# Layer 0's second feed-forward product as 60 slabs and 16 plain quads, with layer 1's memory keys and values right behind it

## The chip, the cores and the metric

One core of one Trainium2 chip. The metric is the device time of one execution in microseconds (us). The time before is the median of three runs.

The engines are PE (TensorE matmuls; PEld are its weight loads), DVE (VectorE), ACT (ScalarE), POOL (GpSimd) and SP (SyncE, which here only issues DMAs).

## The reference

A trunk of two layers over 256 tokens of width 2048, with a memory of 256 tokens, all in float32. What matters here:

```python
for i in range(DEPTH):
    if i == N_A_LAYERS:                       # layer 1
        sk1, sk2, sv = shared_kv(x, kv_norm, w_kv, k_norm, cos, sin)
    u = rms_norm(x, mix_norm[i]) @ w_in[i]
    ...                                       # pooling mixer (0) or differential attention (1)
    mem_out = memory_cross_attention(mem_q, mem, mem_norm[i], w_mem_kv[i], mem_q_norm[i], mem_k_norm[i])
    x = x + jnp.concatenate([token_out, mem_out], axis=-1) @ w_out[i]
    x = x + squared_relu_mlp(rms_norm(x, ffn_norm[i]), w_ff1[i], w_ff2[i])

def squared_relu_mlp(h, w1, w2):              # w1: 2048 x 8192, w2: 8192 x 2048
    z = jax.nn.relu(h @ w1)
    return (z * z) @ w2
```

The keys and values of the memory, `rms_norm(mem) @ w_mem_kv[i]`, need nothing of `x`. The shared keys and values of layer 1 need the `x` that layer 0's feed-forward part leaves.

## The kernel before, in words

**Numbers as high and low halves.** Every float32 operand is split into a rounded high half and the rest. A product is three matmuls: low x high, high x high, high x low. Weights come from HBM in the order of their use. ACT casts a block into `hi_ring`, and DVE subtracts that from the block into `lo_ring` (`_split`, L177 and L180). The rings have six places of 512 columns. `Feed.fill` prepares blocks up to three jobs ahead of PE; `Feed.load` issues the reads some loads ahead, from SP, into `raw` (four buffers, two quads each).

**Forms of a product.** A weight block is 128 x 128; a quad is four of them.
- `a_part`: the weight block is stationary, 256 tokens (high and low half, 512 columns) stream past it, then the low block with 256 columns (L434, L436).
- `wide_step`: a quad streams, and the tokens are stationary: 2 x 3 matmuls of 512 columns (L468 to L470).
- slabs: a slab is two row blocks of the second feed-forward matrix by eight column blocks. It is multiplied by a scheme of seven products in place of eight (L867 to L870), into seven PSUM banks `p`. Its four jobs hold 2, 1, 2 and 2 products. Job 0 takes a block as it is. Then POOL issues a DMA that adds other weights from HBM onto the block in place (`add_right`, L152), and job 1 takes this sum; a sum of L205 gives job 2; after job 2 there is another adding DMA and a sum of L219 for job 3. `product` also takes sums of the inputs (`sit`), made by DVE and ACT from two finished up tiles (`convert`, `combine`, L793 to L804).

**The feed-forward part** (`ffn`, once for a layer). 64 up tiles (`a_part`, 16 blocks each) make `z`, which keeps 16 of 64 row blocks. The slabs run between the up tiles: each job has a due time in up tiles (`tiles_at`), and `due` runs what is due at the start of each tile and after its 4th, 8th and 12th block. The right half of the columns is `g` = 0, the left half `g` = 1. The seven banks hold one side at a time, so the slabs go four on one side, then four on the other, and `swap` copies the banks out and in with ACT (L934, L926). Before, 56 slabs are used: all 32 of the right side, and 24 of the left. The left side is closed in the midst of the up tiles (`close_left`), scaled, and transposed into `resid` (`turn_left`). The rest of the left side, row blocks 48 to 63, follows behind the up tiles as eight down tiles (`down_tile`, `a_part` with 16 blocks each); the last 12 slab jobs run two at a time between them (`last`). `finish_banks` closes the right side and transposes it into `resid`. Each finished block of `resid` is split into `x_kv`.

**Then layer 1:** three tiles of k (`w_kv`), three of v, two of the memory (`mk1`, `mv1`), three of q, and four of the memory's queries with the heads of the attention between. Each tile of k, v, the memory and q is 16 `wide_step`s. The memory's input is read again while k and v run (`mem_again`: four DMAs of four blocks each through `raw`), and split into `mems1`.

**The order of the work.** `at(d, fn)` runs `fn` d ticks later; a tick is one quad, or one job in `last`. The framework that builds the kernel may place an instruction of an engine ahead of others in the code, when its inputs are there; `order` ties those together that have to stay in order.

Of the kernel before, what the change touches and what calls it, by code (L numbers as in the profile page):

```python
# [10 lines left out]
F32 = mybir.dt.float32  # L11
# [89 lines left out]
class Feed:  # L101
# [191 lines left out]
def program(ctx, tc, plan, dry, xT, memT, par, lam, cst, wst, yT):  # L293
# [160 lines left out]

    def wide_step(ps, what, xs, k):
        hi, lo = feed.quad(what)
        x = [(xs[:, k, t * P : t * P + P], xs[:, k, T + t * P : T + t * P + P]) for t in range(2)]
        if what[:2] == ("w_mem_kv", 0) and k < 2:

            for t in range(2):  # L460
                nc.tensor.matmul(ps[t], x[t][0], hi, start=k == 0, stop=False)
            for t in range(2):
                nc.tensor.matmul(ps[t], x[t][1], hi, start=False, stop=False)
            for t in range(2):
                nc.tensor.matmul(ps[t], x[t][0], lo, start=False, stop=False)
        else:
            for t in range(2):
                nc.tensor.matmul(ps[t], x[t][1], hi, start=k == 0, stop=False)  # L468
                nc.tensor.matmul(ps[t], x[t][0], hi, start=False, stop=False)  # L469
                nc.tensor.matmul(ps[t], x[t][0], lo, start=False, stop=k == NK - 1)  # L470
        feed.used(4)
        tick()
# [236 lines left out]

    def later_square(n):  # L710

        if n == 0:
# [17 lines left out]

    def ffn(l, xs, tags, done):

# [20 lines left out]
        cnt = [0]  # L753
        z_done, sit_done, summed_up = set(), set(), set()
        z_free = {j: True for j in range(NK)}
        sit_free = [True] * 4
# [180 lines left out]

        left = {}
        turns = []

        def close_left(j):

# [13 lines left out]
            else:  # L956
                u, v = left["u"], left["v"]
                add(u, u, banks[5])
                sub(v, v, u)
                add(u, u, banks[6])  # L960
            for p in of_job[j]:
                restore(p, 0)
            if j == 3:
                rows = ((left["c11"], 0), (left["c12"], 0), (u, 1), (v, 1))
# [83 lines left out]
        def one_job():  # L1048
# [40 lines left out]
        due(64)  # L1089
        assert len(jobs) == 12 and not turns  # L1090
        feed.loads_ahead = LOADS
# [21 lines left out]

        return last

# [222 lines left out]

    x_in = []
    down = ffn(0, fx, ("S1", "S0"), lambda n: resid_done(n, [(x_in[0], G_KV)], False))  # L1340
# [17 lines left out]

    mems1 = sp.tile([P, NK, 512], F32R, tag="S1", name="mems1")

    def mem_again(p):
        t = wp.tile([P, 4, T], F32, tag="raw", bufs=4, name="memraw1")
        nc.sync.dma_start(t, memT[:, 4 * p : 4 * p + 4, :])
        for k in range(4):
            at(
                6 + 2 * k,
                lambda k=k: split_gain(mems1[:, 4 * p + k, :], t[:, k, :], gcol(G_MEM + 16 + 4 * p + k)),
            )
# [8 lines left out]

    def pair_of_banks(c, name):
        if c % 2:
            return [pp.tile([P, 512], F32, tag="s", bufs=2, name=name) for _ in range(2)]  # L1380
        return [mmt(name) for _ in range(2)]

    c1 = []
    at(12, lambda: c1.extend(columns("x")))
    for c in range(3):
# [20 lines left out]
    mqg1 = mem_gain(1)  # L1406
    ps = pair_of_banks(0, "mk1")
    b_tile(ps, "w_mem_kv", 1, 0, mems1)
    mrow1 = key_rows(ps, mem_c, P)
    ps = pair_of_banks(1, "mv1")  # L1410
    b_tile(ps, "w_mem_kv", 1, 1, mems1)
    cat1 = sp.tile([P, NK, 512], F32R, tag="S1", name="cat1")

    mk1_lo = cat1[:, 12:16, 0:T]
    mv1_lo = cat1[:, 12:16, T : 2 * T].rearrange("p h (a d) -> p h a d", a=2)
    mv1 = tp.tile([P, 2, 512], F32R, tag="rows", bufs=3, name="mv1")
    mk1 = tp.tile([P, 4, T], F32R, tag="rows", bufs=3, name="mk1")
    for t in range(2):
        four = "p (h d) -> p h d"
        hi, v4 = mv1[:, t, :].rearrange(four, h=4), ps[t].rearrange(four, h=4)  # L1420
        split_rows(hi, mv1_lo[:, :, t, :], v4, mem_c[0][:, t : t + 1])
    for i in range(2):
        c = slice(2 * i, 2 * i + 2)
        at(
            2,
            lambda i=i, c=c: turn_rows(mrow1, 2 * i, mk1[:, c, :], gcol(G_MK + 1), mk1_lo[:, c, :]),
        )

    off = [1024]
# [235 lines left out]
```

## Time and profile before

| | |
|---|---|
| median of the runs | 1997.94 us (1997.89 to 1998.28) |
| profiled execution | 1997.9 us, span 1996.1 us |
| granted clock of PE | 1.00 |
| busy: PE, PEld | 1990.8 us (100%), 1704.1 us (85%) |
| busy: DVE, ACT, POOL | 1716.3 us (86%), 1497.9 us (75%), 246.5 us (12%) |
| DMA | 420.10 MB, mean 210 GB/s |

The profile is one execution, and times are counted from its span's start. Ends of matmuls are modelled, so their starts are read. A row of groups has: line, engine, operation, out<-in, count, then busy us and mean ns of one, then the idle time before them and what ended it. A row of the timeline has: start us, us, engine, line, operation, count. A row of DMA issues ends with the KB of each and the us from issue to landing.

Stages: layer 0's up tiles end at about 863 us; the down tiles end at about 926 us; k, v and the memory's tiles follow, and end at about 1101 us.

### The profile page before, as it was taken

The numbers are of one execution on the slowest core, as the hardware profiler recorded it, in microseconds if no ns is written. First come the engines' busy times: TensorE is split into PE (matmuls) and PEld (weight loads), VectorE is DVE, ScalarE is ACT, GpSimd is POOL, SyncE is SP. The second block draws the span as 40 slices with busy tenths as digits, with TensorE's granted clock in tenths as the row PEclk, the third lists the DMA queues.
The fourth block names the chain that finished last, engine by engine and source line by source line (L and its number), as shares of the span: only waits on it lengthen the run. The fifth ranks groups of instructions, "written<-read, shape, count | busy, mean of one in ns | idle before, by whom it ended". The sixth has DMA issues, their size and how long they took to land.

```text
span 1996.1 us, 32052 instructions
## 1 busy us (share of the span) xinstructions
PE 1990.8 (100%) x10534; PEld 1704.1 (85%) x10534; DVE 1716.3 (86%) x3089; ACT 1497.9 (75%) x2791; POOL 246.5 (12%) x291
## 2 busy tenths in 40 slices
PE   9999999999999999999999999999999999999999
PEld 8888888888888888888888888888888888888888
DVE  8888878889989899989765698878889898999987
ACT  7765577787887878778665699567787878878775
POOL 0001311111111111110000000311111111111110
PEclk9999999999999999999999999999999999999999
DMA  8556567888888888765576534657888888888775
GB/s 321 173 192 191 189 200 212 226 227 236 229 229 222 225 236 234 218 189 183 187 234 196 169 127 138 201 186 210 230 219 234 229 227 226 227 234 234 218 216 145
DMA packets 142727, 420.10 MB, mean 210 GB/s; under 512 B 16096, under 2 KB 18784, under 8 KB 142560
## 3 DMA queue, kind: packets, MB, share of 16 engines
q1 hardware_dynamic: 110160, 359.32, 55.3%
q0 software_dynamic: 32256, 58.73, 17.2%
q8 instruction: 82, 1.34, 0.3%
q14 instruction: 85, 0.70, 0.1%
q10 hardware_dynamic: 144, 0.01, 0.0%
HBM read 415.90 MB, written 2.10 MB: 209 GB/s over the span
## 4 chain that ended last, share of the span: by engine, by line
PE 99%; ACT 0%; DVE 0%; issue 0%
PE x_bank L434 25%; PE x_bank L436 12%; PE p L867 9%; PE p L869 9%; PE p L870 9%; PE wo L434 6%; PE wo L436 3%; PE u L434 2%; PE ff L434 2%; PE u L436 1%; PE q L468 1%; PE q L470 1%; PE k L468 1%; PE k L469 1%; PE q L469 1%; PE v L469 1%
## 5 line engine op out<-in xcount | busy, mean ns | idle before, releaser
L177 ACT CAST hi_ring<-raw 128x512 fp32r<-128x512 f32 x1001 | 613.5, 620 | 272.3 <-PE x_bank L434 69.2
L180 DVE TENSOR_TENSOR lo_ring<-raw,hi_ring 128x512 fp32r<-128x512 f32 x1001 | 686.4, 694 | 122.2 <-ACT hi_ring L177 106.2
L434 PE MATMUL x_bank<-fx,hi_ring 128*128 128x512 f32 x1952 | 610.1, 394 | 0.0
L436 PEld LDWEIGHTS x_bank<-fx,lo_ring 128*128 128x128 f32 x1952 | 366.6, 188 | 83.6
L436 PE MATMUL x_bank<-fx,lo_ring 128*128 128x256 f32 x1952 | 383.5, 278 | 0.0
L434 PEld LDWEIGHTS x_bank<-fx,hi_ring 128*128 128x128 f32 x1952 | 319.8, 189 | 24.0
L177 ACT CAST hi_ring<-room 128x1024 fp32r<-128x1024 f32 x224 | 236.0, 1053 | 128.1 <-PE p L869 107.4
L180 DVE TENSOR_TENSOR lo_ring<-room,hi_ring 128x1024 fp32r<-128x1024 f32 x224 | 274.0, 1223 | 37.7 <-ACT hi_ring L177 29.2
L180 DVE TENSOR_TENSOR lo_ring<-slab,hi_ring 128x512 fp32r<-128x512 f32 (+1 forms) x224 | 213.8, 954 | 60.3 <-ACT hi_ring L177 59.8
L177 ACT CAST hi_ring<-slab 128x512 fp32r<-128x512 f32 (+1 forms) x224 | 185.9, 831 | 40.3 <-PE p L869 23.9
L867 PE MATMUL p<-hi_ring,sit 128*128 128x512 f32 x448 | 175.5, 392 | 0.0
L869 PE MATMUL p<-hi_ring,sit 128*128 128x512 f32 x448 | 175.1, 391 | 0.0
L870 PE MATMUL p<-lo_ring,sit 128*128 128x512 f32 x448 | 174.3, 389 | 0.0
L152 POOL DMA_DIRECT2D room<-in_w x112 | 96.7, 863 | 556.3 <-DVE lo_ring L180 435.3
L152 POOL DMA_DIRECT2D slab<-in_w x112 | 96.8, 864 | 529.0 <-DVE lo_ring L180 521.1
L434 PE MATMUL wo<-cat,hi_ring 128*128 128x512 f32 x512 | 161.8, 397 | 0.3 <-DVE rc L405 0.3
L867 PE MATMUL p<-hi_ring,z 128*128 128x512 f32 x336 | 132.1, 393 | 0.0
L869 PE MATMUL p<-hi_ring,z 128*128 128x512 f32 x336 | 131.2, 390 | 0.0
L870 PE MATMUL p<-lo_ring,z 128*128 128x512 f32 x336 | 130.8, 389 | 0.0
L436 PEld LDWEIGHTS wo<-cat,lo_ring 128*128 128x128 f32 x512 | 95.9, 188 | 22.0
L436 PE MATMUL wo<-cat,lo_ring 128*128 128x256 f32 x512 | 101.5, 279 | 0.0
L870 PEld LDWEIGHTS p<-lo_ring,sit 128*128 128x128 f32 x448 | 84.2, 188 | 18.6
(375 smaller groups left out, 3369.7 us busy)
## 6 DMA issues: line engine op xcount, KB each, us to landing
raw<-in_w SPq DMA_DIRECT2D x500, 512.0 KB, 4.4
slab<-in_w SPq DMA_DIRECT2D x112, 512.0 KB, 4.7
room<-in_w SPq DMA_DIRECT2D x112, 256.0 KB, 4.7
slab<-in_w POOLq DMA_DIRECT2D x112, 256.0 KB, 6.6
room<-in_w POOLq DMA_DIRECT2D x112, 256.0 KB, 5.8
memraw<-in_mem SPq DMA_DIRECT2D x5, 512.0 KB, 4.2
resid<-in_x SPq DMA_DIRECT2D x8, 256.0 KB, 5.3
out_y<-resid SPq DMA_DIRECT2D x16, 128.0 KB, 1.9
```

The source lines that it names most:

```text
L152: self.nc.gpsimd.dma_start(t, self.wst[h, :, 0:512], accum_op=ALU.add)
L177: self.last_cast = self.nc.scalar.copy(hi, src)
L180: low = self.nc.vector.tensor_sub(lo, src, hi.bitcast(F32))
L434: nc.tensor.matmul(ps, hi, xs[:, k, :], start=first and c == 0, stop=False)
L436: nc.tensor.matmul(ps[:, T : 2 * T], lo, xs[:, k, 0:T], start=False, stop=last and c == len(ks) - 1,)
L468: nc.tensor.matmul(ps[t], x[t][1], hi, start=k == 0, stop=False)
L469: nc.tensor.matmul(ps[t], x[t][0], hi, start=False, stop=False)
L470: nc.tensor.matmul(ps[t], x[t][0], lo, start=False, stop=k == NK - 1)
L867: nc.tensor.matmul(ps, a[1], hi, start=new, stop=False, **again)
L869: nc.tensor.matmul(ps, a[0], hi, start=False, stop=False, **again)
L870: nc.tensor.matmul(ps, a[0], lo, start=False, stop=end, **again)
```

## The change

In layer 0 (`full`), the left side gets four more slabs, so there are 60: the right side's slabs 24 to 27 come with those of the left side, and the right side's 28 to 31 come last. The due times behind slab 50 follow each other by 0.9 up tiles, not by 1.7. `due` doesn't keep 12 jobs back; what isn't due by the 64th tile runs behind the up tiles, one job after the other (`last_full`). The left side's sums are closed after its slab 27 and kept; the rest of the left side, row blocks 56 to 63, follows behind the slabs as 16 plain quads (`wide_step`) in two pairs of banks, which are added to the kept sums and then scaled and transposed (`turn_side`). The right side is closed by `close_left` too, into `right`. Layer 1's feed-forward part stays as it was.

Behind that, the two tiles of layer 1's memory keys and values come ahead of k and v. Their input is read again while the plain quads run, into the places of `z` (`refill`). `load` returns early where three slabs' halves of one kind are still held.

```diff
@@ Feed.load
             r = self.plan.loads[self.lp]
+            if r[0] == "S" and sum(x[0] == "S" and x[2] == r[2] for x in self.raw) == 3:
+                return
@@ ffn
-        slabs += [(0, i, False) for i in range(24, 32)]
+        if full:
+            slabs += [(0, i, True) for i in range(24, 28)]
+            slabs += [(1, i, False) for i in range(24, 28)]
+            slabs += [(1, i, True) for i in range(28, 28)]
+            slabs += [(0, i, False) for i in range(28, 32)]
+        else:
+            slabs += [(0, i, False) for i in range(24, 32)]
...
-            return p + 8.4 if p <= 50 else 58.4 + 1.7 * (p - 50)
+            return p + 8.4 if p <= 50 else 58.4 + (0.9 if full else 1.7) * (p - 50)
...
-            if end and s + 1 < len(slabs):
-                if g == 1 and i == 23:
+            if s + 1 == len(slabs):
+                if full:
+                    at(1, lambda: close_left(j, right))
+            elif end:
+                if g == 1 and i == (28 - 1 if full else 23):
                     at(1, lambda: close_left(j))
...
-            while len(jobs) > 12:
+            while len(jobs) > (0 if full else 12):
...
+        def turn_side(side, base, h):
+            t4 = pp.tile([P, 2, T], F32, tag="ot"[h % 2], bufs=1, name="ct")
+            sides = ((side["c11"], side["c12"]), (side["u"], side["v"]))
+            ...
+            c = base + 2 * h
+            nc.vector.tensor_add(resid[:, c : c + 2, :], resid[:, c : c + 2, :], t4)
+            at(1, lambda: done(c))
+            at(2, lambda: done(c + 1))
+
+        def last_full():
+
+            while jobs:
+                one_job()
+                tick()
+            rest = range(56, 64)
+            n = len(rest)
+            for d, c, t in ((1, "c11", 0), (2, "c12", 0), (3, "u", 1), (4, "v", 1)):
+                at(d, lambda c=c, t=t: scale_rows(right[c], t))
+            for h in range(4):
+                at((5, 6, 8, 10)[h], lambda h=h: turn_side(right, 8, h))
+            refill(z, n)
+            for c in range(2):
+                ps = pair_of_banks(c, "ff2")
+                for k in rest:
+                    wide_step(ps, ("w_ff2", l, k, c, 4), z, k % NK, (rest[0] % NK, 63 % NK))
+
+                def close(c=c, ps=ps):
+                    for t in range(2):
+                        x = left[(("c11", "c12"), ("u", "v"))[t][c]]
+                        nc.vector.tensor_add(x, x, ps[t])
+                        at(1 + t, lambda x=x, t=t: scale_rows(x, t))
+
+                at(1, close)
+                for e in range(2):
+                    at(5 + e, lambda h=2 * c + e: turn_side(left, 0, h))
+
+        return last_full if full else last
@@ program, between the layers
+    def refill(z, n):
+        mems_in.append(z)
+        def again(p):
+            t = wp.tile([P, 4, T], F32, tag="raw", bufs=RAWS, name="memraw1")
+            nc.sync.dma_start(t, memT[:, 4 * p : 4 * p + 4, :])
+            for k in range(4):
+                at(4 + k, lambda k=k: split_gain(z[:, 4 * p + k, :], t[:, k, :], gcol(G_MEM + 16 + 4 * p + k)))
+        for p, d in enumerate((1, 7, 4 * n // 2 - 3, 4 * n // 2 + 1)):
+            at(d, lambda p=p: again(p))
...
     down()
-    for n in range(NK):
-        at(2 + n // 2, lambda n=n: later_square(n))
+    mems1 = mems_in[0]
+    for i, n in enumerate((8, 9, 10, 11, 12, 13, 14, 15, 0, 1, 2, 3, 4, 5, 6, 7)):
+        at(10 + i, lambda i=i, n=n: later_square(n, i == 0))
+    ps = pair_of_banks(0, "mk1")
+    b_tile(ps, "w_mem_kv", 1, 0, mems1)
+    ...                         # mk1, mv1 and what is made of them, moved from behind v
-    for p in range(4):
-        at(46 + 9 * p, lambda p=p: mem_again(p))
...
-    at(12, lambda: c1.extend(columns("x")))
+    at(2, lambda: c1.extend(columns("x")))
```

More of the change, by code (lines that the diff above doesn't have):

```diff
@@ L453, in c_tile, with wide_step @@
                 tick()
-    def wide_step(ps, what, xs, k):
+    def wide_step(ps, what, xs, k, ends=(0, NK - 1)):
         hi, lo = feed.quad(what)
@@ L467, in wide_step @@
             for t in range(2):
-                nc.tensor.matmul(ps[t], x[t][1], hi, start=k == 0, stop=False)
+                nc.tensor.matmul(ps[t], x[t][1], hi, start=k == ends[0], stop=False)
                 nc.tensor.matmul(ps[t], x[t][0], hi, start=False, stop=False)
-                nc.tensor.matmul(ps[t], x[t][0], lo, start=False, stop=k == NK - 1)
+                nc.tensor.matmul(ps[t], x[t][0], lo, start=False, stop=k == ends[1])
         feed.used(4)
@@ L708, in add_square, with later_square @@
         nc.gpsimd.tensor_add(acc[key], acc[key], sq)
-    def later_square(n):
-        if n == 0:
+    def later_square(n, first):
+        if first:
             acc["x"] = tp.tile([P, T], F32, tag="acc", bufs=1, name="acc")
@@ L728, in resid_done, with pair_of_banks, ffn @@
             add_square("x", resid[:, n, :], n == 0)
-    def ffn(l, xs, tags, done):
+    def pair_of_banks(c, name):
+        if c % 2:
+            return [pp.tile([P, 512], F32, tag="s", bufs=2, name=name) for _ in range(2)]
+        return [mmt(name) for _ in range(2)]
+    def ffn(l, xs, tags, done, refill=None):
         z = sp.tile([P, NK, 512], F32R, tag=tags[0], name=f"z{l}")
@@ L936, in swap, with close_left @@
                 restore(p, g)
-        left = {}
+        left, right = {}, {}
         turns = []
-        def close_left(j):
+        def close_left(j, left=left):
             add, sub = nc.vector.tensor_add, nc.vector.tensor_sub
@@ L960, in close_left @@
                 add(u, u, banks[6])
+            if left is right:
+                return
             for p in of_job[j]:
                 restore(p, 0)
-            if j == 3:
+            if j == 3 and not full:
                 rows = ((left["c11"], 0), (left["c12"], 0), (u, 1), (v, 1))
@@ L1089, in ffn @@
         due(64)
-        assert len(jobs) == 12 and not turns
+        assert full or len(jobs) == 12 and not turns
         feed.loads_ahead = LOADS
@@ L1343, in program @@
     down()
-    for n in range(NK):
-        at(2 + n // 2, lambda n=n: later_square(n))
+    mems1 = mems_in[0]
[3 more added lines that the diff above has]
+    b_tile(ps, "w_mem_kv", 1, 0, mems1)
+    mrow1 = key_rows(ps, mem_c, P)
+    ps = pair_of_banks(1, "mv1")
+    b_tile(ps, "w_mem_kv", 1, 1, mems1)
+    cat1 = sp.tile([P, NK, 512], F32R, tag="S1", name="cat1")
+    mk1_lo = cat1[:, 12:16, 0:T]
+    mv1_lo = cat1[:, 12:16, T : 2 * T].rearrange("p h (a d) -> p h a d", a=2)
+    mv1 = tp.tile([P, 2, 512], F32R, tag="rows", bufs=3, name="mv1")
+    mk1 = tp.tile([P, 4, T], F32R, tag="rows", bufs=3, name="mk1")
+    for t in range(2):
+        four = "p (h d) -> p h d"
+        hi, v4 = mv1[:, t, :].rearrange(four, h=4), ps[t].rearrange(four, h=4)
+        split_rows(hi, mv1_lo[:, :, t, :], v4, mem_c[0][:, t : t + 1])
+    for i in range(2):
+        c = slice(2 * i, 2 * i + 2)
+        at(
+            2,
+            lambda i=i, c=c: turn_rows(mrow1, 2 * i, mk1[:, c, :], gcol(G_MK + 1), mk1_lo[:, c, :]),
+        )
     x_mx = sp.tile([P, NK, 512], F32R, tag="S0", name="x_mx")
@@ L1357, in program @@
     ]
[L1359 to L1368, printed above, removed]
-    for p in range(4):
-        at(46 + 9 * p, lambda p=p: mem_again(p))
     ktab = rope_tables(G_KR, "krope")
@@ L1406, in program @@
     mqg1 = mem_gain(1)
[L1407 to L1427, printed above, removed]
     off = [1024]
```

21 lines of the change are left out of this document (14 added, 7 removed).

## Prediction

> **What bounds the kernel now.** I read the profile's page first: the span, the engines' busy time, and the chain of work that ended last.
>
> ```profile
> span 1996.1 us, 32052 instructions
> PE 1990.8 (100%) x10534; PEld 1704.1 (85%) x10534; DVE 1716.3 (86%) x3089; ACT 1497.9 (75%) x2791; POOL 246.5 (12%) x291
> PE 99%; ACT 0%; DVE 0%; issue 0%
> ```
>
> PE is busy all the time and holds 99% of the chain. A modelled matmul end can hide a wait, so the starts on the timeline of PE decide:
>
> ```profile
> 603.62 0.40 PE L867 MATMUL p<-hi_ring,sit 128*128 128x512 f32 x1
> ...
> 605.67 0.39 PE L867 MATMUL p<-hi_ring,sit 128*128 128x512 f32 x1
> ...
> 606.36 0.62 PE L434 MATMUL x_bank<-fx,hi_ring 128*128 128x512 f32 x2
> ...
> 608.43 0.40 PE L434 MATMUL x_bank<-fx,hi_ring 128*128 128x512 f32 x1
> ```
>
> From 603.62 to 605.67 lie nine 512-wide matmuls of the slab products, one every 0.228 us, though each is printed with 0.39 us. From 606.36 to 608.43 lie three pairs of `a_part` blocks, 0.69 us a pair, 0.345 us a block. PE starts a matmul as soon as the last has streamed, so any time in which a weight block comes late adds to the span. Then the busy time by stages (columns: us, then busy us of PE, PEld, DVE, ACT, POOL, clock, DMA share, GB/s):
>
> ```profile
> 697.10:769.50 72.40, 72.40 (x373) 61.70 (x372) 67.76 (x107) 59.94 (x102) 12.08 (x14) 1.00 0.86 229
> 863.20:916.13 52.93, 52.93 (x288) 45.59 (x287) 49.69 (x88) 39.78 (x71) 3.46 (x4) 1.00 0.63 182
> 1057.00:1101.00 44.00, 44.00 (x196) 36.45 (x195) 25.02 (x42) 24.00 (x42) 0.00 (x0) 1.00 0.60 192
> ```
>
> The first row is seven up tiles with seven slabs: DVE is busy 67.76 of 72.40 us, 94%. The second is the part after the last up tile, where down tiles and the last twelve slab jobs alternate: DVE 49.69 of 52.93. The third is the memory keys and values: DVE 25.02 of 44.00. So PE bounds all three, but DVE, which makes every low half, stands right behind it in the first two. That is where the change works.
>
> **PE's own work.** The change removes 128 `a_part` blocks (eight down tiles of 16): 128 x 0.345 = 44.2 us. It adds four slabs of seven products of three matmuls: 84 x 0.228 = 19.1 us. It adds 16 plain quads of six matmuls; their rate is that of the memory keys, the same `wide_step`:
>
> ```profile
> 1069.99 0.39 PE L468 MATMUL mk<-hi_ring,mems 128*128 128x512 f32 x1
> ...
> 1071.35 0.39 PE L468 MATMUL mk<-hi_ring,mems 128*128 128x512 f32 x1
> ```
>
> 1.36 us a quad, 21.8 us. The 32 transposes that turn the two sides stay 32. PE's work falls by 44.2 - 19.1 - 21.8 = **3.3 us**. If nothing ever came late, this is the whole gain, 0.17% of the span. A gain over 0.2%, 4.0 us, which is about what a measurement of this kernel can tell from no change, needs more than that.
>
> **What DVE has to do for it.** Costs of DVE by form, and three pieces of its timeline that show how close two operations follow:
>
> ```profile
> L180 DVE TENSOR_TENSOR lo_ring<-room,hi_ring 128x1024 fp32r<-128x1024 f32 x224 | 274.0, 1223 | 37.7 <-ACT hi_ring L177 29.2
> L219 DVE TENSOR_TENSOR room<-room,slab 128x512 f32<-128x512 f32 x112 | 77.1, 688 | 1.8
> L776 DVE TENSOR_TENSOR z<-stage,z 128x256 fp32r<-128x256 f32 x128 | 53.6, 419 | 2.7 <-ACT z L772 2.6
> L795 DVE TENSOR_TENSOR room<-room,stage 128x128 f32<-128x128 f32 x64 | 18.5, 289 | 1.5
> 908.04 3.71 DVE L180 TENSOR_TENSOR lo_ring<-raw,hi_ring 128x512 fp32r<-128x512 f32 x6
> ...
> 868.72 1.22 DVE L180 TENSOR_TENSOR lo_ring<-room,hi_ring 128x1024 fp32r<-128x1024 f32 x1
> ...
> 869.85 0.69 DVE L804 TENSOR_TENSOR sit<-room,sit 128x512 fp32r<-128x512 f32 x1
> ```
>
> Six 512-wide operations take 3.71 us, 0.62 us each; a 1024-wide one is followed after 1.13 us. A slab needs three of 1.13 (jobs 0, 2, 3), one of 0.62 (job 1) and the two sums of L205 and L219, 0.62 each: **5.25 us of DVE against 21 x 0.228 = 4.79 us of PE**. Slabs alone would therefore be bound by DVE. An up tile is the reverse: PE 16 x 0.345 = 5.5 us; DVE four low halves and its small operations, 4 x 0.62 + 2 x 0.42 + (4 x 0.29 + 0.62)/2 = 4.2 us. The new pace of 0.9 tile a slab gives PE 0.9 x 5.5 + 4.8 = 9.8 us and DVE 0.9 x 4.2 + 5.25 = 9.0 us, 93%, like the first row of the stages. I cost this stretch at nothing. The extra swap of the seven banks lies there too; its 14 copies on ACT have the whole slab of 9.8 us until their bank is used again. Were that cover gone, a bank would wait for its two copies, about 1.2 us.
>
> **The tail of the slabs.** By the due times (58.4 + 0.9 per step from step 50) the jobs due after tile 64 are job 3 of slab 55 and the jobs of slabs 56 to 59 but for the first jobs of 56 and 57: 15 jobs, 26 products. Before, the last twelve jobs went two at a time between down tiles; now these follow each other with nothing between. PE wants the low half of the last job after 24 products and two matmuls, 24 x 0.684 + 0.46 = 16.9 us. DVE has until then 11 operations of 1.13, four of 0.62 and eight sums of 0.62, 19.9 us, less what stands ready (the preparation runs three jobs ahead; L205, jobs 1 and 2 of slab 56 and a sum, 3.0 us): 16.9 us. On top come three sums of `close_left` (1.9 us), the rest of tile 63 (0.84 us) and the last combinations for the products (1.8 + 0.6 us): 5.1 us. So DVE is late by 16.9 + 5.1 - 16.9 = **5.1 us**. The lower bound is 1 us (DVE goes in further ahead, and small work is pulled before), the upper 8 us: a ring of six places returns a place only when its products are done, and then a cast and a subtraction must pass.
>
> ```profile
> 884.18 0.68 DVE L1001 TENSOR_TENSOR c_b<-c_a,p 128x512 f32<-128x512 f32 x1
> L177 ACT CAST hi_ring<-room 128x1024 fp32r<-128x1024 f32 x224 | 236.0, 1053 | 128.1 <-PE p L869 107.4 <-PE x_bank L434 18.3 <-DVE lo_ring L180 1.1
> raw<-in_w SPq DMA_DIRECT2D x500, 512.0 KB, 4.4
> slab<-in_w POOLq DMA_DIRECT2D x112, 256.0 KB, 6.6
> room<-in_w POOLq DMA_DIRECT2D x112, 256.0 KB, 5.8
> ```
>
> The row at 884.18 is the first sum of `finish_banks`; it runs some tiles ahead of its place in the code. So the order of an engine isn't simply that of the code, and waits can be filled, which is why I don't take the upper bound.
>
> A second thing stands at the end of this stage. Job 3 of a slab needs the accumulating DMA that POOL issues after job 2. In the middle of the slabs a period lies between them; for the last slab only job 3 of the slab before does. The DMA takes 5.8 us, the cast 1.05 us; DVE has L219, one low half of 1.13 us and four sums of `close_right` to do meanwhile, 0.62 + 1.13 + 2.5 = 4.2 us. That leaves 5.8 + 1.05 - 4.2 = 2.6 us; with the 4.4 us of a plain load, in a quieter queue, it leaves 1.2 us. I take **2.0 us**, bounds 0 and 4 (6.6 us, and less to fill it). Before, a pair of jobs and a down tile lay between, and the wait cost nothing.
>
> **The plain quads.** Beside 16 quads (21.8 us) and five turns PE has 24.0 us of work, from these rows:
>
> ```profile
> 916.13 0.87 PE ct L1018 x8
> L330 DVE SCALAR_TENSOR_TENSOR mems<-memraw,param,mems 128x256 fp32r<-128x256 f32 x32 | 14.6, 480 | 3.1 <-ACT mems L412 3.0
> L330 DVE SCALAR_TENSOR_TENSOR x_kv<-resid,param,x_kv 128x256 fp32r<-128x256 f32 x16 | 7.1, 480 | 0.0
> ```
>
> (a turn is four transposes, 0.44 us). DVE gets 16 low halves, 9.9 us, 14 sums of closing and turning (seven, two and five, 8.7 us), eight splits of the memory and eight of x_kv, 16 x 0.48 = 7.7 us: 26.3 us. It is late by 2.3 us more, and has no lead left to hide it: **2.3 us**, bounds 0 (splits wait) and 4. In the 32 quads of the memory that follow, PE has 43.5 us; DVE 19.8 for low halves and some 15 for the rest, so it catches up there.
>
> **The move itself** I cost at nothing. The 32 quads take 1.36 us each wherever they stand, and in the third stage row nothing waits. Four reads of the memory on SP's queue move past the weights of k and v to the plain quads; they take one, at the end two of the four `raw` places, so two are left for weights, 4.4 us a load against 2.7 us a pair of quads, with three quads split ahead. If that cover is short it costs up to 2 us, within the 4 above. The early return in `load` only delays a load that has no place.
>
> **Sum.** -3.3 + 5.1 + 2.0 + 2.3 = +6.1 us. The profiled execution took 1997.9 us (span 1996.1 us and 1.8 us around it) and the median of the runs is 1997.94 us, so both give **2004.0 us**.
>
> **The rivals.**
>
> *The cover holds.* The lateness of DVE is filled from work pulled ahead, and only PE's work counts: 1994.6 us; up to 1998.5 us with a small part of the stalls. For it: the second stage row, 94% DVE without a late matmul, and the row at 884.18. Against it: slabs alone need 5.25 us of DVE for 4.79 us of PE, whatever the order. It decides if the three stalls sum to less than 3.3 us. This is the end on the other side, not slower.
>
> *The accumulating DMA paces the tail.* Two DMAs of 6.6 us lie in the chain of each slab; a period then is half of 6.6 + 5.25, 5.9 us against 4.8, over 3.75 slabs 4 us more than I count: 2008 us, and to 2011.5 us with the upper bounds. Against it: the extra sums partly fill that wait.
>
> *Weight loads count.* 256 loads go and 180 come.
>
> ```profile
> L870 PEld LDWEIGHTS p<-lo_ring,sit 128*128 128x128 f32 x448 | 84.2, 188 | 18.6
> 1206.29 0.48 ACT att L1499
> ...
> 1215.15 0.58 PE st_mq L629 x4
> ```
>
> If loads of 188 ns stood between the matmuls, 76 fewer would save 14.3 us: 1983.6 us. But matmuls start every 0.228 us with a load each, so they lie beside one another. [...]
>
> *Attention gains.* From 1206.29 to 1215.15 the chain leaves PE. If the memory's finishing work, now far ahead, had delayed the heads, a third of these 9 us could come back, for 1992 us. Nothing shows that it did.
>
> **How the numbers follow.** Forecast, 2000 to 2008: 0.52, of which 0.09 lies within 4 us of before. Cover: 0.24. DMA: 0.17. Weight loads: 0.02. Attention: 0.05. Slower by over 0.2% is 0.43 + 0.17 = 0.60, within it 0.09 + 0.24 = 0.33, faster 0.07. The range goes from the low end of the cover, 1994.5, to 2011.5 and leaves out the two fast rivals and some of the DMA's top. The forecast's own range is 2000 to 2008.
>
> **What would show it.** Right: between the last up tile and the first plain quad PE's matmul starts show gaps that sum to some 7 us, ended by low halves, one of 1 to 3 us ahead of the last job; some 2 us more within the plain quads; the memory and k quads at 1.36 us. Wrong: slab jobs at 0.228 us a matmul through the tail (the cover), gaps at every job 1 or 3 ended by a DMA (the second rival), or gaps in k and v.

## Result and the profile after

The changed kernel takes 2004.43 us (median of 8 runs, 2003.07 to 2005.44); the kernel before takes 1998.25 us beside it (8 runs, 1997.89 to 1998.54). The ratio is 1.0031, interval 1.0021 to 1.0040: slower by 6.2 us, 0.3%. The profiled execution of the changed kernel took 2004.71 us. Line numbers of the changed kernel stand two to eight above those of before in the functions that matter here: the cast is L179, the low half L182, the slab's sums L207 and L221, its adding DMA L154, the slab products L875, L877 and L878, the quads L470 to L472.

The page of the changed kernel, the lines for span, busy time and chain:

```profile
span 2003.0 us, 31909 instructions
PE 1992.4 (99%) x10458; PEld 1697.4 (85%) x10458; DVE 1718.7 (86%) x3077; ACT 1500.8 (75%) x2807; POOL 253.5 (13%) x299
PE 97%; DVE 2%; ACT 1%; issue 0%; DVEq 0%; ACTq 0%
```

The span grew by 6.9 us, and 3% of the chain now lies on DVE and ACT, where there was nothing to speak of. PE's printed busy time even grew by 1.6 us, though PE has less to do. A gap stretches the printed matmul beside it (0.50 or 0.73 us in place of 0.39 and 0.62 in the timeline below), so the busy time doesn't show what was lost. The stages show where it went (same columns as in the prediction; the last up tile ends at 875.5, the first plain quad is at 900.35, the memory's keys start at 927.87 and k at 973.5):

```profile
862.00:876.00 14.00, 14.00 (x73) 11.93 (x72) 14.00 (x23) 11.23 (x19) 1.75 (x3) 1.00 0.89 258
876.00:900.35 24.35, 20.29 (x75) 12.95 (x74) 23.02 (x35) 17.56 (x28) 6.01 (x7) 1.00 0.55 109
900.35:927.87 27.52, 27.03 (x129) 21.70 (x128) 25.66 (x47) 22.75 (x48) 0.00 (x0) 1.00 0.60 181
927.87:973.50 45.63, 45.26 (x202) 36.34 (x200) 45.00 (x97) 38.13 (x83) 0.00 (x0) 1.00 0.71 236
```

Before the tail (first row) DVE has no free moment, 14.00 of 14.00 us, while PE still loses nothing. In the tail of the slabs (second row) PE starts 75 matmuls in 24.35 us; at 0.228 us each they would take 17.1 us. In all, 84 slab matmuls (28 products) follow the last up tile: the fifteen jobs that are left, and ahead of them the first job of slab 57, which `due(64)` starts there. The two rows behind it are almost full.

What PE waited for from 862 to 935 (line, releaser: us in all, times, longest):

```profile
PE p L878 <- DVE lo_ring L182: 2.8, 4, 1.1
PE p L875 <- ACT hi_ring L179: 1.4, 3, 0.7
PE mk L472 <- DVE lo_ring L182: 0.3, 1, 0.3
```

and the timeline of PE through the end of the tail:

```profile
889.86 0.73 PE L878 MATMUL p<-lo_ring,z 128*128 128x512 f32 x2 [0.60 <-DVE lo_ring L182]
891.66 0.49 PE L878 MATMUL p<-lo_ring,sit 128*128 128x512 f32 x1 [1.08 <-DVE lo_ring L182]
...
896.33 0.50 PE L878 MATMUL p<-lo_ring,sit 128*128 128x512 f32 x1 [0.79 <-DVE lo_ring L182]
...
897.74 0.40 PE L877 MATMUL p<-hi_ring,sit 128*128 128x512 f32 x1
898.85 0.50 PE L875 MATMUL p<-hi_ring,z 128*128 128x512 f32 x1 [0.72 <-ACT hi_ring L179]
...
900.35 0.39 PE L470 MATMUL ff<-hi_ring,z 128*128 128x512 f32 x1
...
902.71 0.40 PE L471 MATMUL ff<-hi_ring,z 128*128 128x512 f32 x1
903.55 0.50 PE L875 MATMUL p<-hi_ring,z 128*128 128x512 f32 x1 [0.45 <-ACT hi_ring L179]
```

The brackets hold only the part of a gap that the modelled matmul ends leave over; from 897.74 to 898.85 are 1.11 us where 0.23 would do. I therefore count stalls by starts: over all matmuls, the time from one start to the next less 0.230 us (512 wide), 0.116 (256 wide) or 0.110 (a transpose), added up with its sign, so that a stretch without a wait comes out near zero (from 600 to 950 us the kernel before starts the next one on average 0.230 us after a 512-wide matmul and 0.115 after a 256-wide one). "Gaps" means this count from here on. Matmuls at a lower clock count in it too; in this profile the clock is 1.00 in all four rows. Between the last up tile and 901 us the gaps come to 7.3 us, from there to the memory's keys 1.0 us, of which 0.8 lie around 902 to 903.55, before the last slab job, and in the first 22 us of the memory 0.9 us. From 863 to 950 us the kernel before has none to speak of, below 0.1 us in all.

DVE at the same place, the only idle moments it has in the tail:

```profile
896.92 1.22 DVE L182 TENSOR_TENSOR lo_ring<-room,hi_ring 128x1024 fp32r<-128x1024 f32 x1 [0.64 <-ACT hi_ring L179]
...
898.83 1.23 DVE L182 TENSOR_TENSOR lo_ring<-room,hi_ring 128x1024 fp32r<-128x1024 f32 x1 [0.69 <-ACT hi_ring L179]
...
903.53 1.23 DVE L182 TENSOR_TENSOR lo_ring<-room,hi_ring 128x1024 fp32r<-128x1024 f32 x1 [0.47 <-ACT hi_ring L179]
```

Up to 896.3 us DVE is without an idle moment; PE's gaps up to there come to 5.8 us, and most of them are ended by a low half. After that PE, ACT and DVE wait together, for casts that stand behind the last slabs' adding DMAs (no_add_dma below shows it): some 2.4 us.

### The profile page after: what moved, and what is told of

It reads as the page before. It is cut to its first block, busy times and chain, and to the rows that moved or that the text cites. A ratio compares the mean times of both kernels' runs of the same rounds, so it can differ in the third digit from the quotient of the medians.

```text
span 2003.0 us, 31909 instructions
## 1 busy us (share of the span) xinstructions
PE 1992.4 (99%) x10458; PEld 1697.4 (85%) x10458; DVE 1718.7 (86%) x3077; ACT 1500.8 (75%) x2807; POOL 253.5 (13%) x299
## 4 chain that ended last, share of the span: by engine, by line
PE 97%; DVE 2%; ACT 1%; issue 0%; DVEq 0%; ACTq 0%
PE x_bank L436 24%; PE x_bank L438 12%; PE p L875 9%; PE p L877 9%; PE p L878 9%; PE wo L436 6%; PE wo L438 3%; PE u L436 2%; PE ff L436 1%; PE u L438 1%; PE k L470 1%; PE k L472 1%; PE v L472 1%; PE v L470 1%; PE k L471 1%; PE v L471 1%
## 5 line engine op out<-in xcount | busy, mean ns | idle before, releaser
L179 ACT CAST hi_ring<-raw 128x512 fp32r<-128x512 f32 x985 | 604.5, 620 | 260.3 <-PE wo L436 58.6
L182 DVE TENSOR_TENSOR lo_ring<-raw,hi_ring 128x512 fp32r<-128x512 f32 x985 | 676.4, 694 | 120.1 <-ACT hi_ring L179 105.6
L179 ACT CAST hi_ring<-room 128x1024 fp32r<-128x1024 f32 x232 | 244.4, 1054 | 156.5 <-PE p L877 128.4
L182 DVE TENSOR_TENSOR lo_ring<-room,hi_ring 128x1024 fp32r<-128x1024 f32 x232 | 283.6, 1223 | 56.6 <-ACT hi_ring L179 51.6
L182 DVE TENSOR_TENSOR lo_ring<-slab,hi_ring 128x512 fp32r<-128x512 f32 (+1 forms) x232 | 221.4, 954 | 44.8 <-ACT hi_ring L179 41.1
L179 ACT CAST hi_ring<-slab 128x512 fp32r<-128x512 f32 (+1 forms) x232 | 192.5, 831 | 28.5 <-PE p L877 16.8
L878 PE MATMUL p<-lo_ring,sit 128*128 128x512 f32 x464 | 180.5, 390 | 2.3 <-DVE lo_ring L182 2.2
L875 PE MATMUL p<-hi_ring,sit 128*128 128x512 f32 x464 | 182.3, 393 | 0.3 <-ACT hi_ring L179 0.2
L877 PE MATMUL p<-hi_ring,sit 128*128 128x512 f32 x464 | 181.4, 391 | 0.0
L154 POOL DMA_DIRECT2D slab<-in_w x116 | 100.4, 865 | 567.4 <-DVE lo_ring L182 546.4
L154 POOL DMA_DIRECT2D room<-in_w x116 | 100.1, 863 | 515.9 <-DVE lo_ring L182 413.7
L875 PE MATMUL p<-hi_ring,z 128*128 128x512 f32 x348 | 136.8, 393 | 1.2 <-ACT hi_ring L179 1.2
L878 PE MATMUL p<-lo_ring,z 128*128 128x512 f32 x348 | 135.4, 390 | 0.7 <-DVE lo_ring L182 0.6
L877 PE MATMUL p<-hi_ring,z 128*128 128x512 f32 x348 | 135.9, 390 | 0.0
L878 PEld LDWEIGHTS p<-lo_ring,sit 128*128 128x128 f32 x464 | 87.1, 188 | 23.1 <-DVE lo_ring L182 4.0
```

The costliest lines, as they stand in the source:

```text
L154: self.nc.gpsimd.dma_start(t, self.wst[h, :, 0:512], accum_op=ALU.add)
L179: self.last_cast = self.nc.scalar.copy(hi, src)
L182: low = self.nc.vector.tensor_sub(lo, src, hi.bitcast(F32))
L875: nc.tensor.matmul(ps, a[1], hi, start=new, stop=False, **again)
L877: nc.tensor.matmul(ps, a[0], hi, start=False, stop=False, **again)
L878: nc.tensor.matmul(ps, a[0], lo, start=False, stop=end, **again)
```

## The experiments

All times are medians, with the ratio to the kernel before as run on the same chip. Its median is 1998.00 us beside no_sums, no_add_dma, mem_back and quads_56, 1997.94 beside pace12 and the three with sums on POOL, 1998.08 beside the hybrids. A difference to the changed kernel is the difference of the medians. The intervals of the ratios overlap or touch for differences of up to about 4 us, so that the traces have to carry the reading there. In kernels with a `TAIL` line the line numbers are one to four higher.

**no_sums: the tail without the slab's two sums**

```diff
+TAIL = range(56, 60)
@@ the sum of L207
+            if p[1] in TAIL:
+                return True
@@ the sum of L221
-            add(rb[:, 0:512], rb[:, 0:512], ra[:, 512:1024])
+            if p[1] not in TAIL:
+                add(rb[:, 0:512], rb[:, 0:512], ra[:, 512:1024])
```

> Leaves out the eight sums that DVE makes for slabs 56 to 59 (L207 and L221), so part of those weights is wrong; everything else of the changed kernel stays. Theory (DVE's own work makes the slab tail late): DVE has 8 x 0.62 = 5.0 us less to do in a stretch without idle time, so the time falls by 4 to 5 us, from 2004.4 to about 2000. Rival (the adding DMAs pace the tail): the sums only lie behind the landing; at most 0.6 us falls for one slab, 1 to 2 us in all, 2002.5 to 2003.5.

2000.27 us, ratio 1.0011 (1.0002 to 1.0021): 4.2 us less than the changed kernel, for eight sums of 0.62 us, 5.0 us of DVE. A stage row (876 to 898 us) and PE's waits of this kernel:

```profile
876.00:898.00 22.00, 18.99 (x75) 13.02 (x74) 18.89 (x27) 16.83 (x27) 5.46 (x7) 1.00 0.63 125
```

```profile
PE p L879 <- ACT hi_ring L180: 2.7, 4, 1.3
PE p L882 <- DVE lo_ring L183: 0.3, 1, 0.3
```

DVE is busy 18.89 of 22.00 us, and PE's wait for low halves falls from 2.8 to 0.3 us. The gaps from 855 to 928 us fall from 8.2 to 5.1. The wait for casts rises from 1.4 to 2.7: with DVE relieved, the adding DMAs seem to be next. Leaving a sum out also shortens the chain of one block (sum, cast, low half); that DVE has no idle moment up to 896.3 us in the changed kernel is what speaks for its work, and not this chain.

**no_add_dma: the tail without the adding DMAs**

```diff
+TAIL = range(56, 60)
@@ add_right
+        if n in TAIL:
+            return
```

> Leaves out the eight adding DMAs of slabs 56 to 59, so part of those weights is missing; all casts, subtractions and sums stay. Theory (DVE's work): only the waits at the end of the tail go, which DVE shows as 0.64, 0.69 and 0.47 us of idle time: 1 to 2 us less, 2002.5 to 2003.5. Rival (the adding DMAs pace the tail): the gaps between the slab jobs go, 5 to 7 us less, 1997.5 to 1999.5.

2002.36 us (2001.84 to 2003.21), ratio 1.0021 (1.0012 to 1.0031): 2.1 us less, 0.1 us below the theory's range and far from the rival's. PE's waits here on the slab products:

```profile
PE p L881 <- DVE lo_ring L185: 2.6, 4, 1.1
```

No wait for a cast is left on them, and the wait for DVE stays (2.6 us, 2.8 in the changed kernel). So these are two causes, and DVE is the larger. The clock is halved for 3.4 us of the tail in this profile (see the last section), but the seven runs whose mean clock is 1.000 have nearly the same median, 2002.33 us.

**quads_56: shorter tail, more plain quads**

56 slabs and 32 plain quads, twelve jobs left behind the last up tile. The memory's splits overwrite row blocks here that the second pair of columns still reads, so part of the computation is changed.

```diff
-            slabs += [(0, i, True) for i in range(24, 28)]
-            slabs += [(1, i, False) for i in range(24, 28)]
...
-            return p + 8.4 if p <= 50 else 58.4 + (0.9 if full else 1.7) * (p - 50)
+            return p + 8.4 if p <= 50 else 58.4 + 1.7 * (p - 50)
...
-            while len(jobs) > (0 if full else 12):
+            while len(jobs) > 12:
...
-            rest = range(56, 64)
+            rest = range(48, 64)
...
```

> Leaves the four extra slabs out: 56 slabs at the old pace of 1.7 tiles, the left side closed after its slab 23, and 32 plain quads for row blocks 48 to 63 behind a run of the last 12 jobs with nothing between. Memory tiles as in the changed kernel. PE has 0.7 us less to do than before. Theory (DVE's work): 21 products, 14.4 us of PE, against some 16 us of DVE, so late by 2 to 4 us: 1999.5 to 2001.5. Rival (not the slabs but the missing down tiles between the jobs cost it all): the 7 us of the tail stay, 2004 to 2006.

2000.72 us, ratio 1.0013 (1.0004 to 1.0023). The tail of this kernel:

```profile
862.00:880.00 18.00, 15.82 (x65) 11.27 (x64) 16.75 (x25) 13.47 (x21) 3.40 (x4) 1.00 0.49 102
```

The gaps of the tail halve, to about 3.5 us, with DVE at 16.75 of 18.00 us. Twelve slab jobs back to back lose less than sixteen; the 32 plain quads behind them lose nothing (PE is busy 45.00 of 45.00 us from 880 to 925). Plain quads are not the trouble, slab jobs in a row are. The kernel before has the same 56 slabs and the same twelve jobs left, but between down tiles, and has no gaps there. So with the same slabs it decides what stands beside the jobs; the memory's place, which differs too, leaves the tail alone, as mem_back shows.

**pace12: the slab jobs brought forward**

```diff
+            if full and p > 30:
+                return 38.4 + 0.95 * (p - 30) if p <= 50 else 57.4 + 0.9 * (p - 50)
...
-            while len(jobs) > (0 if full else 12):
+            while len(jobs) > 12:
+                if full and not ready(*jobs[0][1:]):
+                    break
@@ last_full, ahead of each job
+                while not ready(*jobs[0][1:]):
+                    tick()
```

> One change of schedule: steps 30 to 50 follow each other by 0.95 tile in place of 1.0, so the slabs come in one tile earlier, and 12 jobs in place of 15 are left behind the up tiles. Nothing is left out. Theory (DVE's work): the up tiles had DVE at 90% to 94%, so three jobs move into its idle time at no cost; they hold some 3.5 us of DVE and 3.4 us of PE less in the tail, whose lateness falls by 1.5 to 3 us: 2001.5 to 2003. Rival (a fixed latency at the end of the slabs): 2004 to 2005.

2002.92 us (2002.41 to 2003.38), ratio 1.0024 (1.0014 to 1.0034): 1.5 us less. The gaps from 876 to 928 us fall from 8.3 to 5.1, but 1.8 us of new ones appear at 600 to 660 us, where the denser schedule begins. Twelve jobs in a row in the tail, in place of sixteen, don't make it free.

**mem_back: the memory's keys and values behind v again**

```diff
-        for k in range(NK):
-            wide_step(ps, [(w, l, k, n, 1) for n in blocks], xs, k)
+        for k in (*range(8, NK), *range(8)):
+            wide_step(ps, [(w, l, k, n, 1) for n in blocks], xs, k, (8, 7))
...
-            refill(z, n)
...
+    for p in range(4):
+        at(46 + 9 * p, lambda p=p: mem_again(p))
...                                   # mk1 and mv1 stand behind v, as before
```

> Undoes the move: layer 1's memory tiles stand behind v again with their input read while k and v run; k and q take row blocks 8 to 15 ahead of 0 to 7, since the left side of x is finished last. The 60 slabs and 16 plain quads stay. Theory (the move costs nothing by itself, the slab tail costs all): 2003 to 2005, at most 1 us less since the memory's splits leave the plain quads. Rival (the refill in the plain quads costs the 2.3 us of the prediction's sum, or the move's reads delay weights): 2001 to 2002.5.

2002.82 us (2002.70 to 2005.33), ratio 1.0026 (1.0016 to 1.0035): 1.6 us less, between the two ranges. The gaps of the tail are nearly the same (7.1 us against 7.3, with 3.4 us at half clock in this profile, see the last section); those of 928 to 950 us go from 0.9 to none. So the place of the memory bears no part of the tail's loss, and costs about 1 us of its own, as far as the overlapping intervals let one say.

**pool_sums, both, both_mb: sums of the tail on POOL**

```diff
+TAIL = range(55, 60)                  # both, both_mb: range(53, 60)
-            add(rb[:, 0:512], rb[:, 0:512], ra[:, 512:1024])
+            eng = self.nc.gpsimd if p[1] in TAIL else self.nc.vector
+            eng.tensor_add(rb[:, 0:512], rb[:, 0:512], ra[:, 512:1024])
```

`both` adds this to pace12, `both_mb` to pace12 with the memory behind v.

> One change to the changed kernel: the sum of L221 of slabs 55 to 59 is made by POOL, which is idle most of the tail, in place of DVE. Theory (DVE's work): DVE loses 5 x 0.62 = 3.1 us in the stretch without idle time, so 2 to 3 us less than 2004.4: 2001.5 to 2002.5. Rival (latency of the adding DMAs, or of cast and subtraction, and not DVE's work): no gain, or slower, since POOL takes about 2 us for a sum of 512 (1.03 us for 256 in the profile of before) and issues the adding DMAs too: 2004 to 2006.

> The schedule of the run with 12 jobs left and the sums of L221 of slabs 53 to 59 on POOL. Theory: both gains add, 4 to 6 us less than 2004.4: 1998.5 to 2000.5. Rival: what remains is latency, and the second gain is lost: 2001.5 to 2003.

> The same as the run before it, with the memory tiles behind v again as in the run that undid the move (k and q take row blocks 8 to 15 first). Theory: the move is worth less than 1 us either way, so 1998 to 2000.5. Rival (the memory's splits hold up the plain quads once the tail is short): 1996 to 1998.

All three missed: 2008.56 us (1.0051, 1.0034 to 1.0068), 2006.48 (1.0042, 1.0027 to 1.0057) and 2006.51 (1.0043, 1.0028 to 1.0058). In pool_sums five sums of 0.62 us left DVE, and the kernel became 4 us slower in place of some 2 us faster. The timelines of POOL and DVE in pool_sums:

```profile
878.86 4.69 POOL L223 TENSOR_TENSOR room<-room,slab 128x512 f32<-128x512 f32 x1
883.50 0.87 POOL L155 DMA_DIRECT2D slab<-in_w  x1
...
885.50 1.59 POOL L223 TENSOR_TENSOR room<-room,slab 128x512 f32<-128x512 f32 x1
...
897.50 1.62 POOL L223 TENSOR_TENSOR room<-room,slab 128x512 f32<-128x512 f32 x1
...
903.05 1.58 POOL L223 TENSOR_TENSOR room<-room,slab 128x512 f32<-128x512 f32 x1
```

```profile
885.16 2.22 DVE L786 TENSOR_TENSOR z<-stage,z 128x256 fp32r<-128x256 f32 x1
...
897.69 1.99 DVE L208 TENSOR_TENSOR room<-slab,room 128x512 f32<-128x512 f32 x1
902.62 3.10 DVE L183 TENSOR_TENSOR lo_ring<-room,hi_ring 128x1024 fp32r<-128x1024 f32 x1 [0.48 <-ACT hi_ring L180]
```

The last three of the five POOL sums each lie beside a DVE operation, and that operation takes 1.3 to 1.9 us longer: 2.22 us against the 0.42 that the prediction's rows have for its form, 1.99 against 0.69, 3.10 against 1.22. They end 0.29, 0.56 and 1.09 us after the POOL sums do, near their own usual lengths. Together these three take 5.0 us more, where five sums of 0.62, 3.1 us, were taken away: the work left DVE, its time didn't. The sum at 878.86 itself takes 4.69 us, and POOL issues its next adding DMA only behind it, at 883.50; in the changed kernel this one goes out at 881.90. The gaps from 876 to 928 us grow to 13.1 us. Part of them is the clock, which is halved for 10.2 us of this stretch:

```profile
887.90:894.73 6.83, 5.93 (x13) 3.93 (x13) 5.03 (x10) 3.39 (x6) 0.88 (x1) 0.50 0.68 153
901.50:904.91 3.41, 3.41 (x9) 2.44 (x8) 2.93 (x2) 2.08 (x3) 2.19 (x2) 0.51 0.22 35
```

The run with the least of this (mean clock 0.999, against 0.997 in the profiled one) took 2007.18 us, still 2.8 us above the changed kernel. How much of the 4 us goes to the longer DVE operations, to the later adding DMAs and to the clock, no run separates.

**hybrid, hybrid26, hybrid15: the last slab jobs between down tiles again**

These stand on the kernel before: 60 slabs (58 in hybrid26), the rest of the rows as eight `a_part` down tiles of 8 (12) blocks in place of plain quads, with the last slab jobs between the tiles; the memory stays behind v. hybrid15 keeps the changed kernel's due times from step 50 and leaves 15 jobs; there the left side is turned ahead of its scaling, so part of the computation is changed.

```diff
-            ks = range(3 * NK, 4 * NK)
+            ks = range(3 * NK + (8 if l == 0 else 0), 4 * NK)
...
-        slabs += [(0, i, False) for i in range(24, 32)]
+            slabs += [(0, i, True) for i in range(24, 28)]
+            slabs += [(1, i, False) for i in range(24, 28)]
+            slabs += [(0, i, False) for i in range(28, 32)]
...
+            if full and p > 30:
+                return 38.4 + 0.95 * (p - 30) if p <= 50 else 57.4 + 0.9 * (p - 50)
...
-                    some(ends[n][0])
+                    some((4, 2, 2, 2, 2, 0)[n] if full else ends[n][0])
...
```

> A version that the runs point to: the 60 slabs of the change with the schedule that leaves 12 jobs, but row blocks 56 to 63 of the left side as eight half down tiles (a_part, eight blocks each) in the one free bank, between the last jobs (four ahead of the first tile, then two ahead of each of four); memory tiles behind v, as before the change. Nothing is left out. PE has 44.2 - 19.1 - 64 x 0.345 = 3.0 us less to do than before. Theory (DVE's work in the slab tail is the loss): the jobs' 14.4 us now stand beside 22.1 us of tiles that need little of DVE; DVE has some 39 us against 36.5, late by 2 to 3 us or less: 1995.5 to 1998.5. Rival (more slabs than 56 always cost more than they save): 2000 or more.

> The same with 58 slabs: the left side has two more than before, and row blocks 52 to 63 stay as eight down tiles of 12 blocks. Nothing is left out. PE has 1.6 us less to do than before (half of 3.0 us, since half the slabs move). Theory: DVE has some 44 us against 47.5 us of PE in the tail, so nothing is late: 1996 to 1997.5. Rival: as above, 1999 or more.

> The 60 slabs with the half down tiles, with the due times of the change and 15 jobs left, four ahead of the first tile, then three, three, three and two. Nothing is left out. Theory (DVE's work): 17.8 + 22.1 = 39.9 us of PE against some 43 us of DVE: 1997 to 2000, about 1 us above the version that leaves 12. Rival: no difference between the two, since the end of the last slab is what counts.

2004.54 us (1.0032, 1.0020 to 1.0045), 2003.74 (1.0029, 1.0017 to 1.0040) and 2008.77 (1.0051, 1.0037 to 1.0065): all missed. The stages of the kernel before, and then those of hybrid, through the last up tiles and the down tiles:

```profile
844.00:863.00 19.00, 19.00 (x105) 16.36 (x104) 16.06 (x29) 13.57 (x24) 2.50 (x3) 1.00 0.74 204
863.00:926.00 63.00, 63.00 (x347) 54.47 (x346) 59.06 (x109) 47.76 (x88) 3.46 (x4) 1.00 0.58 171
```

```profile
857.00:876.00 19.00, 19.00 (x98) 15.94 (x97) 19.00 (x31) 16.59 (x28) 3.45 (x4) 1.00 0.83 236
876.00:945.00 69.00, 64.64 (x324) 51.39 (x323) 67.13 (x128) 59.34 (x118) 4.31 (x5) 1.00 0.53 150
```

PE's wait in hybrid from 927 to 950 us, the beginning of k:

```profile
PE k L472 <- DVE lo_ring L182: 1.6, 3, 0.9
```

Before, DVE enters the last stretch with 3 us to spare in 19 and is busy 59.06 of 63 us. In hybrid it has none (19.00 of 19.00), then 67.13 of 69, and the lateness goes on into k. Down tiles between the jobs only spread the waits: gaps of 5.0 us from 876 to 928 and 2.4 us in k up to 950. A further 1.0 us of hybrid and 3.6 of hybrid26 lie at 600 to 660 us, where the denser schedule begins. Of the 3.6 some 1.6 are the clock, which is halved there for 3.4 us in the profiled execution, the slowest of the six:

```profile
634.00:645.00 11.00, 9.38 (x38) 7.25 (x37) 7.65 (x12) 7.88 (x13) 1.51 (x2) 0.84 0.67 172
```

hybrid15, with fifteen jobs left, loses most: 13.3 us of gaps from 876 to 950, with two stretches of 3.4 us at half clock among them. So the order of the jobs helps only where DVE has time to spare: with 56 slabs the down tiles between the jobs hide what quads_56 loses, with 60 they no longer do.

No version of these is faster than the kernel before. mem_back and pace12 together, not run, come to an estimated 2004.4 - 1.6 - 1.5 = 2001.3 us if the two add, still slower.

## Why the prediction was right

Slower was the forecast, 2004.0 us; it is 2004.43. Its sum was -3.3 + 9.4 us of stalls. In the profiled executions the gaps of the changed kernel exceed those of before by 9.65 us over the whole span; 0.56 of it lie before 600 us, where both kernels do the same and most of the other traces have none of it. So 9.1 us belong to the change, and the remainder of the span, 6.9 - 9.65 = -2.8 us, is PE's own work. Term by term:

- **PE's own work**, -3.3 predicted, about -2.8 found. With 0.230 us a matmul, as in the count of the gaps, the prediction's own sum is 44.3 - 19.3 - 22.1 = 2.9 us.
- **DVE late in the tail**, +5.1, and **the wait for the adding DMA**, +2.0: together 7.1 predicted, 7.3 + 0.8 = 8.1 found; by place, 5.8 us up to 896.3 and some 2.4 behind. no_sums shows that DVE's work is the larger part (4.2 us come back for 5.0 us of sums), no_add_dma that the DMA is the smaller (2.1 us). The DMA's wait doesn't stand ahead of the last job alone, as I had it, but ahead of the last two: 1.11 - 0.23 = 0.9 us at 898.85 and 0.84 - 0.23 = 0.6 us at 903.55. The wait for the last job is short because plain-quad matmuls run from 900.35 to 902.71, ahead of it. That this could be filled from the next stage I had not seen.
- **DVE's lead.** I gave DVE 3.0 us of work done ahead as the tail begins, and costed the dense stretch before it at nothing. PE loses nothing there, but DVE, 14.00 of 14.00 us busy, can't get as far ahead. The first of the fifteen jobs starts on PE at 876.94 us, and of the four operations that I took for done (a sum of L207, the low halves of jobs 1 and 2 of slab 56, a sum of L221) two are done then and the third has begun:

```profile
874.23 0.68 DVE L207 TENSOR_TENSOR room<-slab,room 128x512 f32<-128x512 f32 x1
...
875.43 0.68 DVE L182 TENSOR_TENSOR lo_ring<-slab,hi_ring 128x512 fp32r<-128x512 f32 x1
...
876.57 1.22 DVE L182 TENSOR_TENSOR lo_ring<-room,hi_ring 128x1024 fp32r<-128x1024 f32 x1
...
878.04 0.68 DVE L221 TENSOR_TENSOR room<-room,slab 128x512 f32<-128x512 f32 x1
```

That is 0.62 + 0.62 + 0.37 = 1.6 us of lead, 1.4 us short, which more than covers the tail's 1 us over the forecast. Whether the ring's six places add to it stays open, since a longer ring was not tried.
- **The plain quads**, +2.3 predicted. This term was too large: 0.2 us are left once the last job's wait is taken off. DVE was busy 25.66 us there, near the 26.3 of the sum, but the last slab job and its wait lie in the same stretch, so that it is 27.5 us long and not 24.0. quads_56, with 32 of them, loses nothing there either.
- **The move itself**, 0 predicted. About 1 us: gaps of 0.9 us in the memory's first 22 us, which mem_back takes away. In the prediction I named a price of up to 2 us for reads that come late, and then took none. The largest gap, 0.47 us at 930.18, is ended by a low half of DVE and not by a read. DVE doesn't catch up there, as I had said: it is busy 45.00 of 45.63 us, where I gave it some 35 of 43.5. In the second half of the memory's stretch the quads run as said, 1.36 us each:

```profile
949.70 0.39 PE L470 MATMUL mk<-hi_ring,z 128*128 128x512 f32 x1
...
951.06 0.39 PE L470 MATMUL mk<-hi_ring,z 128*128 128x512 f32 x1
```

The direction and the mechanism, DVE's work in the tail and the last adding DMA, were right. That the total came within 0.4 us is luck: quads and move are 1.2 us below the forecast, the tail is 1 us above and PE's own work gains 0.5 us less.

The rivals: **the cover holds** falls, by 9 us of gaps. **The adding DMA paces the tail** falls: without those DMAs 2.1 us come back where it needed 5 to 7. (Its sum took both adding DMAs at 6.6 us; the row of the second has 5.8.) **Weight loads count** falls with the sum; 76 loads fewer saved nothing beyond the matmuls (PE's own work fell by about 2.8 us, where the matmuls alone give 2.9). (Its 1983.6 us also left out the 3.3 us of PE's work.) **Attention gains** falls: from 1103 to about 1270 us the gaps are 3.8 us in both kernels.

## What to carry to other kernels

Where PE has no gap and a second engine is 94% busy, price every swap of form in both engines' time: here slabs save PE work against blocked tiles (four come to 84 x 0.228 = 19.1 us, the 64 `a_part` blocks they stand for to 64 x 0.345 = 22.1), but one costs DVE 5.25 us for 4.79 us of PE, and they were free only where slack from other work lay beside them. Interleaving with lighter work hid that debt where DVE had time to spare in the stretch (the kernel before, DVE 59.06 of 63 us and no gaps, against some 3.5 us of them in quads_56); where it had none, interleaving or an earlier start only moved it (hybrid, with 5.0 us of gaps in the tail and 2.4 in k; pace12, with 1.8 us of new ones at 600 to 660), and of what was tried only less DVE work in the tail brought more than 2.1 us back (no_sums 4.2, quads_56 3.7). And look whether the helper engine is free together with the engine it is to relieve, before work is handed to it: in pool_sums 3.1 us of sums left DVE, and three of its other operations took 5.0 us more.

## What the runs showed of the hardware

**POOL beside DVE.** The rows of pool_sums above: three 128x512 sums on POOL print 1.6 us (POOL's spans are rough), and the DVE operations beside them take 1.3 to 1.9 us longer than their usual 0.42 to 1.22. The sum at 878.86 takes 4.69 us itself. Beside it DVE's five operations from 878.85 to 882.99 keep their usual time (1.21, 1.21, 0.68, 0.68 and 0.67 us), and the next, at 882.96, takes 1.68 us in place of 1.22. So in these rows now one engine and now the other takes longer while both work; why, no run shows.

**Stretches at half clock.** In mem_back, behind a gap of 1.07 us in the tail, matmuls start 0.43 us apart in place of 0.23. Its stage row (the third figure from the right is the granted clock) and its timeline:

```profile
891.60:895.01 3.41, 3.41 (x9) 2.67 (x10) 3.41 (x5) 1.95 (x3) 0.86 (x1) 0.50 0.45 74
```

```profile
891.10 0.50 PE L878 MATMUL p<-lo_ring,sit 128*128 128x512 f32 x1 [1.07 <-DVE lo_ring L182]
891.44 0.65 PE L875 MATMUL p<-hi_ring,sit 128*128 128x512 f32 x1
891.88 0.63 PE L877 MATMUL p<-hi_ring,sit 128*128 128x512 f32 x1
892.30 0.63 PE L875 MATMUL p<-hi_ring,sit 128*128 128x512 f32 x1
```

The clock is 0.50 for 3.41 us; seven such matmuls cost 7 x 0.2 = 1.4 us where they stand. The profiles of no_add_dma, both, both_mb and hybrid26 have one such stretch of 3.4 us too, that of hybrid15 has two, and that of pool_sums has one of 6.8 us and one of 3.4. The profile of the changed kernel, with a gap of the same size at 891.66, kept the clock at 1.00. So of two executions with a gap of about 1 us at that place one had a stretch at half clock behind it and the other none; what lowers the clock, no run shows.

Such a stretch shows in the mean clock of a run: the profiled runs have 0.999 with one of 3.4 us, 0.998 with two, and 0.997 with 10.2 us in all. It doesn't explain why the changed kernel's runs spread over 2.4 us where those of before spread over 0.65: seven of its eight runs have a mean clock of 1.000, and they cover the whole spread, 2003.07 to 2005.44 us. In mem_back the six runs at 0.999 are no longer than the four at 1.000 (medians 2002.80 and 2002.96 us), so there the 1.4 us don't show in the whole time. A likely reason, which no run tests, is that DVE, which PE waits for around that stretch, goes on in the meantime. In hybrid15 the time does rise as the clock falls: 2006.34 and 2007.61 us at 0.999, 2008.77 and 2008.86 at 0.998, 2010.52 at 0.997.
